# Attention of a hybrid trunk layer: value scale from column norms, bias shift as its own work, and a new table of work

## The chip, the cores and the metric

The kernel runs on one core of a Trainium2 chip. The metric is the device time of one execution in microseconds (us). The kernel before was timed three times: 1098.44, 1096.51 and 1096.65 us, a median of 1096.65 us. A separate profiled execution took 1097.14 us.

## The reference, cut to what matters

One layer is computed for two groups of tokens with shared weights: 128 context tokens and 512 latent tokens, 640 together, 1024 channels wide. The change lies in the attention of this layer:

```python
def block_attention(q, k, v):
    B, N, H, D = q.shape
    KV = k.shape[2]
    G = H // KV
    ...
        s = jnp.einsum('bqkgd,btkd->bkgqt', qblk, k).astype(jnp.float32) * scale
        p = jax.nn.softmax(s, axis=-1).astype(v.dtype)
        return jnp.einsum('bkgqt,btkd->bqkgd', p, v)
```

There are 16 query heads and 4 key/value heads of 64 channels. Context queries read the 128 context keys; latent queries read 512 latent keys and 128 cached ones. Before this stands the first projection (`u @ w_in`, with a normalisation of q and k per head and a rotary turn); behind it stand the output projections, a gated convolution and a feed-forward part. Those stages are not changed.

## The kernel before, in words

Every large product is made in three matmuls of rounded parts (high by high, high by low, low by high). The program runs in stages: a prologue that makes the keys and values of all 640 tokens; the attention; then the mixing stage, the feed-forward part and the output. Only the attention stage is changed. In the profile it begins at about 57.5 us, when the last products of keys and values end, and ends at about 243.1 us, when the first matmul of the next stage starts.

**Works.** The attention stage is written as a list of small pieces, each of them a `work` with a name, an engine, the works it must follow and the "rooms" it holds (a bank of PSUM, a slot of SBUF). The long string `PLAN` at the head of the file is the order: each entry is the number of a work, a letter for the engine where a work can run on one of several ("a" is the first), and digits that pick its rooms. `follow` issues the works in exactly this order, so each engine's instruction queue is fixed by the table; an engine never passes over an instruction that waits. `POOL_WAY` is a string of 32 digits; a "1" sends one subtraction (P2 of the second half of a step) to GpSimd (POOL), a "0" to VectorE (DVE).

**The pieces that the prediction speaks of**, by their names in the code:

- `q{g}{t}.{c}`: a quarter of the query projection for key/value head g and token tile t, six matmuls (line 687). `rot`, `sq`, `sum`, `factor`, `add`, `norm` (lines 818 to 865) make the rotary turn and the normalisation of a tile of q or k on DVE, ScalarE (ACT) and POOL; `turn` transposes it on PE (894, 1018), and `hi` and `lo` split the result (900, 903, 1020, 1022).
- `hi {u}` and `lo {u}`: the split of a weight unit (799, 804); each has two `lo` halves, on DVE or POOL.
- The **value scale**: every value channel is divided by a number of its own so that it fits 16-bit floats, and multiplied back at the end. `vmax` (910) takes the largest magnitude of each of the 256 channels over 768 tokens per partition; `v turn` (917) transposes; `v col` (921 to 923) takes the maximum over partitions and its reciprocal; `v spread` (930) and `v row` (932) spread it over all partitions; `v back` and `v un` (939, 945 to 947) keep the inverse; `v scale` (959), `v hi` (965) and `v lo` (968) make the 16-bit parts of the values, in thirds. All three `v hi` wait for all three `v scale`, since the parts lie on the values' own memory.
- A **step** n (36 of them, for g, t and half of the four heads): `s{n}` makes scores on PE (1057) in one PSUM "area" per head (three areas exist, A of two banks each); `max{n}.{h}` (1104, with the shift of the bias at 1106 for the second head) on DVE; `exp` (1109) and `P1` (1115) on ACT; `P2` (1120, 1122) on POOL or DVE; `T` (1126) a transposing DMA from the SP queue; `pv{n}` (1143, 1151) the product with the values on PE. On the POOL way `exp` writes to an SBUF slot E, so the area is free after `exp`; on the DVE way the area stays held until `P2` has read it.
- `R`, `O`, `AH`, `AL` (1163 to 1173) finish a pair of steps. `gate0` and `gate1` are products of the next stage that fill PE at the end.

Of the kernel before, what the change touches and what calls it, by code (L numbers as in the profile page):

```python
# [52 lines left out]
49a 113a 66a 119a 353a5 63a 50a 61a 64b 120a 109a01 39a 138a 121a 40a 110a 359a21 62a 100a 124a1 204a 114b 140a 115a1 135a0 360a
101a 116a2 139b 117a 361a 136a 125a 365a 102a1 206b 275a 362a2 141a 122a12 103a3 366a0 142a 126a 104a 205a 354a1 144a2 363a 123a
281a 367a4 372a01 143a0 127a 355a0 364a0 145a 356a 146a 128a4 378a 357a 151a0 129a0 147a 358a 379a1 152a 130a 368a 373a 389a21
380a3 370a 374a 381a 369a1 148a1 395a 153a 375a1 390a 149a1 154a 382a2 396a0 376a 157a0 150a 391a 402a10 377a3 155a21 397a0 400a
383a 156a 158a 371a1 392a2 408a 398a 403a 164a0 409a1 393a 159a 404a 399a4 165a 410a4 413a 419a02 160a 405a3 394a5 411a 384a
406a 425a 407a0 161a3 385a2 166a 420a 162a3 426a0 386a 167a 412a1 163a 387a 421a 432a21 388a 168a10 427a1 430a 401a1 169a 433a
170a1 422a0 428a 438a 434a 177a0 423a 439a1 429a2 178a 171a 435a2 443a 172a 449a01 440a3 436a 424a3 173a 414a 455a 441a 437a4
450a 456a0 174a4 179a 175a2 415a1 176a 457a4 180a 416a 442a5 462a12 417a 458a 181a02 451a 418a 183a2 463a 431a1 452a1 182a 459a0  # L60
453a 464a 190a0 468a 465a0 454a1 479a0 184a 469a1 466a 444a 185a 480a 470a2 467a2 186a 491a21 473a 445a0 460a 481a 446a 471a
191a 497a 447a 482a 472a3 492a 192a 483a3 498a0 448a 193a 484a 493a 187a1 485a4 194a21 504a10 188a0 499a4 502a 189a 195a 196a0
461a1 505a 500a 494a1 510a 506a 474a 495a 501a5 511a 207a0 197a 475a2 515a 198a 507a0 476a 496a0 208a 477a 508a 512a2 199a 478a
210a 521a21 509a1 513a 276a 211a 486a1 527a 212b 514a2 200a2 487a0 522a 201a1 277b 213a 528a1 488a 202a 214a 489a 875a 278b
529a3 490a 534a10 215a1 523a 530a 879a 216a1 503a1 532a 524a4 535a 531a3 540a 536a 516a 525a 541a0 223a0 217a 517a1 545a 218a
542a1 518a 551a20 526a4 519a 537a0 219a 520a 224a 557a 543a 220a1 552a 225a 558a1 538a 221a3 544a0 226a 559a2 222a 564a01 229a2
560a 553a 539a5 227a02 533a1 565a 554a3 228a 570a 566a 561a1 236a0 555a 571a0 237a 230a 567a4 562a 575a 231a 581a21 556a2 572a1
568a 232a 546a 582a 573a 569a3 587a 583a 233a2 238a 547a0 234a2 548a 588a1 239a 235a 574a4 549a 594a01 240a21 584a0 550a 589a2
241a 585a 563a1 242a0 590a 595a 586a0 611a2 600a 596a 249a0 591a5 612a 601a0 576a 243a 597a3 592a 605a 244a 602a4 598a 250a
577a2 245a 613a 599a1 578a 623a10 603a 251a 579a 629a 615a1 604a2 580a 252a 630a1 616a 246a1 255a1 624a 617a3 636a20 247a0 631a0  # L70
253a10 625a 632a 642a 593a0 626a2 248a 637a 606a 643a 254a 633a4 634a 256a 638a 627a 262a1 257a 607a1 647a 628a0 614a 644a3 608a
263a 258a 609a 645a 639a4 259a3 264a 610a 260a1 646a5 640a 282a 618a0 261a 653a02 284a 641a1 619a2 620a 283b 265a 621a 659a 883a
622a 660a0 654a 279a0 268a2 666a12 876a 266a00 269a 267a 655a 635a1 672a 270a 661a1 877a 648a 656a0 667a 271a 673a1 280a 878b
664a 657a 649a1 674a2 272a4 650a 658a2 285a 662a 273a3 651a 274a 668a 286a 652a 887a 675a 683a02 288a0 677a 663a3 669a3 287a2
289a 295a1 684a 290a 888a0 689a 685a 291a 296a 676a0 670a 690a0 889a 686a4 694a 696a12 691a0 687a 671a4 692a 297a 697a 292a2
702a 698a 298a 688a1 890a 293a2 299a12 699a1 294a 891a 301a1 300a 700a 703a1 693a5 308a1 302a 892a 707a 713a01 704a2 303a 678a0
304a 719a 705a 714a 720a0 665a 701a0 715a 726a21 679a0 706a4 724a 716a3 680a 309a 732a 681a 721a4 682a 310a 733a 717a 722a 305a0
311a 727a 718a2 306a0 734a0 743a0 307a 314a2 735a 695a0 728a 723a3 312a01 729a1 708a 744a 313a 736a1 730a 745a 321a1 315a 737a
755a12 316a 731a5 709a2 746a 747a2 710a 322a 317a 761a 711a 712a 323a 762a1 756a 318a0 324a 748a 763a3 319a1 768a20 749a0 764a
325a20 757a 320a 327a0 766a 758a4 738a0 774a 326a 765a4 769a 775a0 725a 759a 770a 750a1 328a 760a1 739a1 779a 329a 771a0 740a  # L80
785a01 751a2 772a 741a 330a 776a1 742a 773a5 331a4 791a 777a 334a0 332a3 786a 792a1 335a 333a 778a2 787a 752a 798a12 793a2 796a
336a 753a 804a 794a 880a 754a 337a 805a0 799a 881b 795a3 767a1 338a10 788a3 806a4 789a 882b 780a 340a1 800a 790a0 341a 807a
815a20 781a1 809a 801a0 782a 893a0 342a 339b 808a1 783a 816a 884a 894a 821a 343a 817a 885b 784a 895a 822a1 802a 344a1 886b 896a
818a1 803a4 826a 345a2 828a10 819a 823a2 346a 897a 820a2 824a 797a1 834a 829a 835a0 898a0 825a5 830a 845a20 836a3 839a 810a
831a4 846a 837a 832a 847a 899a 851a 833a0 811a2 900a 848a0 812a 901a 852a1 849a 838a3 813a 858a10 856a 853a1 814a 902a 854a
850a1 827a1 864a 859a 865a 903a2 855a4 860a 840a 866a2 869a 861a4 867a 904a 841a1 862a 911a 868a2 905a 842a 843a 863a5 906a 844a
857a0 907a 908a 870a 909a 871a0 872a 873a 910a 874a
"""
POOL_WAY = "11111111101111111011111011111110"
# [20 lines left out]
def trunk_layer(ctx, tc, x_prompt, x_sample, cache_k, cache_v, c, c_ctx, w_ada, b_ada, g_pre1, g_post1, g_pre2,  # L110
# [614 lines left out]
    with tc.tile_pool(name="att", bufs=1) as at:  # L725
# [147 lines left out]
        for t in range(NT):  # L873
# [28 lines left out]
            def k_lo(kh=kh, kl=kl, pk=pk):  # L902
# [3 lines left out]


        vsum, vsq = vcol[:, 0:2], vcol[:, 2:4]
        vz = Room(any_of("X", NX))
        big = work("vmax", "DVE", lambda: V.tensor_reduce(out=slot(XS, vz), in_=VV.rearrange("p s c -> p c s"), axis=AX.X, op=ALU.max,  # L910
                                                                          apply_absolute_value=True), list(v_copies.values()), [vz])
        pv_ = Room(ANY)

        def v_turn():
            p = at_bank(pv_, 256)
            for i in range(2):
                PE.transpose(p[:, i * 128:(i + 1) * 128], slot(XS, vz)[:, i * 128:(i + 1) * 128], ident)
# [1437 lines left out]
```

## Time and profile before

| what | value |
|---|---|
| median of three runs | 1096.65 us |
| the profiled execution, its own time | 1097.14 us |
| its span, first to last instruction | 1095.3 us |
| TensorE (PE) matmul busy | 1075.9 us (98%) |
| DVE busy | 858.6 us (78%) |
| ACT busy | 580.9 us (53%) |
| POOL busy | 130.4 us (12%) |
| granted TensorE clock, mean | 0.997 |
| attention stage | about 57.5 to 243.1 us of the span |

Times in the views are counted from the first instruction of the program. A row of the timeline gives start, duration, engine, line, operation, written tile <- read tiles, and behind it in brackets idle time of the engine and who ended it. A row of stretches gives busy time of each engine in a stretch (and the number of instructions), then the granted TensorE clock, the mean share of the DMA engines that was busy, and GB/s. A row of groups gives busy time and the mean duration in ns of instructions with one line and shape. A busy PE is not PE at its peak: the ends of its matmuls are modelled, and two that follow each other overlap.

### The profile page before, as it was taken

Reading aid. Unit: us, or ns where it says so; the run is one execution under the profiler, and the core shown is the slowest. Engines: PE = TensorE matmul, PEld = TensorE weight load, DVE = VectorE, ACT = ScalarE, POOL = GpSimd, SP = SyncE. Lnnn points to the kernel's source line nnn. Section 1 sums busy time; section 2 is a strip of 40 time slices with the busy share of each in tenths; the row PEclk is TensorE's granted clock in tenths of the full one; section 3 lists DMA queues with packets and bytes.
Section 4 is the critical chain, followed back from the end, with each engine's and each line's share of the span. In section 5 each row is a group of like instructions: output and inputs, shape, how many; then the busy total and the mean of one; then the engine's idle time right before and its main releaser. Section 6 shows DMA issues by size and latency. Waiting matters only on the chain.

```text
span 1095.3 us, 20378 instructions
## 1 busy us (share of the span) xinstructions
PE 1075.9 (98%) x8133; PEld 998.4 (91%) x8133; DVE 858.6 (78%) x1316; ACT 580.9 (53%) x1047; POOL 130.4 (12%) x161
## 2 busy tenths in 40 slices
PE   8999999999999999999999999999999999999997
PEld 6788888889999999999999789999999999998886
DVE  5698988856479889987488468889989988989544
ACT  5458987862344454445423266655556455545442
POOL 1077655620000000000000021000000000000001
PEclk9999999999999999999999999999999999999999
DMA  9828999898234333233445634234434433335722
GB/s 321 246 71 145 181 172 169 153 179 223 72 101 123 109 97 92 78 97 97 130 142 190 196 135 136 91 100 128 129 113 128 139 103 107 122 102 194 268 82 96
DMA packets 245613, 152.18 MB, mean 139 GB/s; under 512 B 94602, under 2 KB 224134, under 8 KB 245518
## 3 DMA queue, kind: packets, MB, share of 16 engines
q1 hardware_dynamic: 245406, 150.84, 50.3%
q8 instruction: 64, 1.05, 0.4%
q14 instruction: 31, 0.25, 0.1%
q10 hardware_dynamic: 112, 0.04, 0.0%
HBM read 117.39 MB, written 11.44 MB: 118 GB/s over the span
## 4 chain that ended last, share of the span: by engine, by line
PE 78%; ACT 1%; DVE 1%; DMA 0%; SPq 0%; issue 0%; POOL 0%; DVEq 0%; ACTq 0%
PE b L1255 46%; PE b L232 10%; PE b L234 10%; PE b L233 10%; PE b L1874 1%; DMA PT<-P 0%; PE b L287 0%; SPq L1126 0%; PE b L1724 0%; DVE marks L1104 0%; ACT P L1115 0%; ACT E L1109 0%; PE s L687 0%; PE b L350 0%; ACT s L1109 0%
## 5 line engine op out<-in xcount | busy, mean ns | idle before, releaser
L1255 PE MATMUL b<-ZBr,whi 128*128 128x320 f32 x688 | 152.2, 309 | 0.0
L1255 PE MATMUL b<-MT,whi 128*128 128x320 f32 x608 | 134.2, 309 | 0.0
L1255 PEld LDWEIGHTS b<-ZBr,whi 128*128 128x128 f32 x688 | 115.0, 188 | 0.1
L1255 PE MATMUL b<-ZBr,wlo 128*128 128x320 f32 x344 | 106.2, 309 | 0.0
L1255 PEld LDWEIGHTS b<-MT,whi 128*128 128x128 f32 x608 | 101.6, 188 | 0.0
L1255 PE MATMUL b<-MT,wlo 128*128 128x320 f32 x304 | 94.0, 309 | 0.0
L1242 ACT ACTIVATE whi<-SUM 128x1024 fp32r<-128x1024 f32 x40 | 42.2, 1055 | 78.4 <-DVE SUM L1789 75.9
L1819 DVE SCALAR_TENSOR_TENSOR Y<-C,cffn,Y 128x642 f32<-128x642 f32 x88 | 77.9, 885 | 0.9
L1255 PE MATMUL b<-ZBT,whi 128*128 128x320 f32 x320 | 71.0, 309 | 0.0
L1255 PE MATMUL b<-UL,whi 128*128 128x320 f32 x228 | 70.8, 311 | 0.0
L1255 PE MATMUL b<-UH,wlo 128*128 128x320 f32 x228 | 70.1, 307 | 0.0
L1242 ACT ACTIVATE whi<-WB 128x1024 fp32r<-128x1024 f32 x38 | 40.1, 1055 | 55.9 <-DVE WB L1356 55.9
L1255 PE MATMUL b<-UH,whi 128*128 128x320 f32 x228 | 69.7, 306 | 0.0
L1246 DVE TENSOR_TENSOR wlo<-raw,whi 128x1024 fp32r<-128x1024 f32 (+1 forms) x51 | 50.4, 1020 | 21.8 <-ACT whi L1242 21.8
L198 DVE TENSOR_TENSOR wlo<-raw,whi 128x1024 fp32r<-128x1024 f32 (+1 forms) x31 | 34.2, 1103 | 41.1 <-ACT whi L197 40.6
L1255 PEld LDWEIGHTS b<-ZBr,wlo 128*128 128x128 f32 x344 | 64.6, 188 | 0.0
L1263 ACT ACTIVATE p<-b 128x320 f32<-128x320 f32 x78 | 34.2, 439 | 54.8 <-PE b L1255 53.0
L1255 PEld LDWEIGHTS b<-MT,wlo 128*128 128x128 f32 x304 | 57.1, 188 | 0.0
L1255 PEld LDWEIGHTS b<-ZBT,whi 128*128 128x128 f32 x320 | 54.2, 188 | 1.5
L1104 DVE TENSOR_REDUCE marks<-s 128x1 f32<-128x640 f32 x64 | 51.5, 816 | 4.4 <-PE s L1057 4.4
L1246 DVE TENSOR_TENSOR wlo<-WB,whi 128x1024 fp32r<-128x1024 f32 x38 | 46.5, 1223 | 8.7 <-ACT whi L1242 8.6
L1242 ACT ACTIVATE whi<-raw 128x1024 fp32r<-128x1024 f32 (+1 forms) x51 | 43.5, 892 | 18.0 <-PE b L234 10.3
(422 smaller groups left out, 3220.4 us busy)
## 6 DMA issues: line engine op xcount, KB each, us to landing
raw<-in_w_in_dram SPq DMA_DIRECT2D x48, 512.0 KB
RAW<-in_w_up_dram SPq DMA_DIRECT2D x40, 512.0 KB
raw<-in_w_down_dram SPq DMA_DIRECT2D x22, 512.0 KB
actd<-Y SPq DMA_DIRECT2D x18, 321.0 KB
ada<-in_w_ada_dram SPq DMA_DIRECT2D x10, 512.0 KB
XT<-in_w_ada_dram SPq DMA_DIRECT2D x9, 512.0 KB
raw<-in_w_att_out_dram SPq DMA_DIRECT2D x8, 512.0 KB
raw<-in_w_conv_out_dram SPq DMA_DIRECT2D x8, 512.0 KB
```

The source lines that it names most:

```text
L198: V.tensor_tensor(out=lo[:, :n], in0=raw, in1=hi[:, :n].bitcast(F32), op=ALU.subtract)
L232: PE.matmul(out, ah, bh, start=start, stop=False)
L233: PE.matmul(out, ah, bl, start=False, stop=False)
L234: PE.matmul(out, al, bh, start=False, stop=stop)
L1104: V.tensor_reduce(out=mk[:, h:h + 1], in_=s_of(), axis=AX.X, op=ALU.max, negate=True)
L1242: S.activation(to[0], raw, AF.Copy)
L1246: V.tensor_tensor(out=lo, in0=raw, in1=hi.bitcast(F32), op=ALU.subtract)
L1255: PE.matmul(out, p[:, ws], q[:, k, :], start=start and k == 0 and n == 0, stop=stop and k == 3 and n == 2, skip_group_check=True)
L1263: S.activation(t, pair[j][b], AF.Copy)
L1819: V.scalar_tensor_tensor(out=y, in0=crows(j)[i][:, d:d + NACT], scalar=cffn[:, 44 * d + o:44 * d + o + 1], in1=y, op0=ALU.mult, op1=ALU.add)
L1874: PE.matmul(dn["pms"][t], acts(k)[1][i][:, c0:c0 + 128], w[h], start=False, stop=n == 2 and k == NJ - 1)
```

## The change

Three things are changed, all in the attention stage.

1. The value scale of a channel is no longer the reciprocal of its largest magnitude but of the root of its sum of squares. `vmax` and `v turn` go. In their place stand three `v square` on ACT (each squares a third of the values, 512 elements per partition, into a slot P), three `v total` on PE (each four matmuls of 128 channels against two columns of ones), a smaller `v col` on DVE that adds the six sums of a channel and keeps them off zero, and `v factor` on POOL, a power of -0.5. The reciprocal in `v col` goes. Everything from `v spread` on stays.
2. The shift of the bias is a work of its own, `shift{n}`, on DVE; `exp{n}.1` follows it.
3. `PLAN` is a new table for the 949 works there are now (912 before), with new choices of engines and rooms, and `POOL_WAY` sends 26 subtractions to POOL (28 before).

```diff
-POOL_WAY = "11111111101111111011111011111110"
+POOL_WAY = "11111111101111011111111101111000"
...
-        vz = Room(any_of("X", NX))
-        big = work("vmax", "DVE", lambda: V.tensor_reduce(out=slot(XS, vz), in_=VV.rearrange("p s c -> p c s"), axis=AX.X, op=ALU.max,
-                                                                          apply_absolute_value=True), list(v_copies.values()), [vz])
         pv_ = Room(ANY)
-
-        def v_turn():
-            p = at_bank(pv_, 256)
-            for i in range(2):
-                PE.transpose(p[:, i * 128:(i + 1) * 128], slot(XS, vz)[:, i * 128:(i + 1) * 128], ident)
-        vt = work("v turn", "PE", v_turn, [big], [pv_, vz])
+        tops = []
+        for i in range(3):
+            vz = Room(any_of("P", NP_))
+
+            def square(i=i, vz=vz):
+                S.activation(slot(PS, vz).bitcast(F32)[:, 0:512].rearrange("p (s c) -> p s c", s=2), VV[:, 2 * i:2 * i + 2, :], AF.Square)
+
+            def total(i=i, vz=vz):
+                p, x = at_bank(pv_, 24), slot(PS, vz).bitcast(F32)
+                for k in range(4):
+                    c = 4 * i + k
+                    PE.matmul(p[:, 2 * c:2 * c + 2], x[:, k * 128:(k + 1) * 128], ones[:, 0:2], start=True, stop=True, skip_group_check=True)
+            a = work(f"v square {i}", "ACT", square, [v_copies[t] for t in ((1,), (2, 3), (4, 0))[i]], [vz])
+            tops.append(work(f"v total {i}", "PE", total, [a], [vz, pv_]))
 
         def v_col():
-            V.tensor_reduce(out=vsum, in_=at_bank(pv_, 256).rearrange("p (i c) -> p i c", i=2), axis=AX.X, op=ALU.max)
+            p = at_bank(pv_, 24).rearrange("p (s i two) -> p i s two", i=2, two=2)[:, :, :, 0]
+            V.tensor_reduce(out=vsum, in_=p, axis=AX.X, op=ALU.add)
             V.tensor_scalar(out=vsum, in0=vsum, scalar1=1e-30, scalar2=None, op0=ALU.max)
-            V.reciprocal(vsq, vsum)
-        vc = work("v col", "DVE", v_col, [vt], [pv_])
+        vc = work("v col", "DVE", v_col, tops, [pv_])
+        vc = work("v factor", "POOL", lambda: G.tensor_tensor(out=vsq, in0=vsum, in1=mhalf[:, :2], op=ALU.pow), [vc])
...
                         V.tensor_reduce(out=mk[:, h:h + 1], in_=s_of(), axis=AX.X, op=ALU.max, negate=True)
-                        if h:
-                            V.tensor_scalar(out=mk[:, 1:2], in0=mk[:, 1:2], scalar1=SHIFT * math.log(2), scalar2=None, op0=ALU.add)
+
+                    def shifted(mk=mk):
+                        V.tensor_scalar(out=mk[:, 1:2], in0=mk[:, 1:2], scalar1=SHIFT * math.log(2), scalar2=None, op0=ALU.add)
                     mx = work(f"max{n}.{h}", "DVE", most, [sc], [ar[h]])
+                    if h:
+                        mx = work(f"shift{n}", "DVE", shifted, [mx])
```

The table moves works on every engine. Three places matter for the prediction. In the rows below stand the line, the operation, the written tile <- the read tiles, and the size; the changed file's lines are 2 higher up to `v scale`'s chain, 8 higher in the chain and the scores, and 11 higher behind the shift.

**VectorE, around the value column (`v col`).** Before, `vmax` (L910) comes tenth in the stage, and `v col` (L921 to L923) three works behind it:

```order
L847 TENSOR_REDUCE ssqs<-Z_731 128x4
L910 TENSOR_REDUCE X_732<-VV 128x256
L847 TENSOR_REDUCE ssqs<-Z_729 128x4
L855 TENSOR_TENSOR PT_724<-P_721,rk 128x512
L921 TENSOR_REDUCE vcol<-s_102_840 128x2
L922 TENSOR_SCALAR vcol<-vcol 128x2
L923 RECIPROCAL vcol<-vcol 128x2
```

Now `v col` (L929, L930) stands behind the rotation, the sums and the additions of the third query tile:

```order
L824 TENSOR_TENSOR X_734<-s_94_755,tabq 128x256
L825 TENSOR_TENSOR QF_737<-s_94_755,tabq 128x256
L845 TENSOR_TENSOR QF_736<-QF_736,X_733 128x256
L849 TENSOR_REDUCE ssqs<-Z_730 128x4
L1030 TENSOR_TENSOR QT_738<-s_98_808,QT_738 128x256
L867 TENSOR_TENSOR QF_736<-QF_736,rq 128x256
L845 TENSOR_TENSOR QF_737<-QF_737,X_734 128x256
L929 TENSOR_REDUCE vcol<-s_103_914 128x2
L930 TENSOR_SCALAR vcol<-vcol 128x2
```

What moved: the column of sums is the 29th work of VectorE in the stage, where it was the 13th.

**GpSimd, the value chain.** Before, GpSimd does one `v scale` (L959) and one `v lo` (L968) of three:

```order
L855 TENSOR_TENSOR PT_727<-P_720,rk 128x512
L959 TENSOR_TENSOR P_722<-VV,vrow 128x512
L843 TENSOR_TENSOR QF_737<-QF_737,X_732 128x256
L850 TENSOR_TENSOR rq<-ssqs,mhalf 128x4
L968 TENSOR_TENSOR VV<-P_721,VV 128x512
```

Now it does the power (L932), all three `v scale` (L967) and all three `v lo` (L976):

```order
L867 TENSOR_TENSOR QF_737<-QF_737,rq 128x256
L932 TENSOR_TENSOR vcol<-vcol,mhalf 128x2
L852 TENSOR_TENSOR rq<-ssqs,mhalf 128x4
L967 TENSOR_TENSOR P_722<-VV,vrow 128x512
L967 TENSOR_TENSOR P_719<-VV,vrow 128x512
L967 TENSOR_TENSOR P_718<-VV,vrow 128x512
L845 TENSOR_TENSOR QF_735<-QF_735,X_732 128x256
L976 TENSOR_TENSOR VV<-P_719,VV 128x512
L976 TENSOR_TENSOR VV<-P_718,VV 128x512
L976 TENSOR_TENSOR VV<-P_722,VV 128x512
```

What moved: two thirds of the scaling and of the low parts went from VectorE to GpSimd, in a row.

**TensorE, from `s2` to `s3`.** The scores write PSUM areas (`s_...` with a number). Before, `s3` writes one area that `s2` had (s_102_840) and one that it had not, and a turn and projection pieces (L687) stand between them:

```order
L1057 MATMUL s_102_840<-KH,QT_739 128x320
L1018 MATMUL s_104_927<-ident,QF_736 128x128 x2
L687 MATMUL s_94_755<-whi_829,UH 128x256
L687 MATMUL s_94_755<-wlo_830,UH 128x256
L687 MATMUL s_94_755<-whi_829,UL 128x256
L1057 MATMUL s_104_927<-KH,QT_741 128x320
L1057 MATMUL s_102_840<-KH,QT_741 128x320
```

Now `pv0` and a turn alone (L1154, L1162, L1026) stand between `s2` and `s3`, and `s3` writes both areas of `s2`:

```order
L1065 MATMUL s_103_914<-KH,QT_740 128x320
L1065 MATMUL s_99_839<-KH,QT_740 128x320
L1154 MATMUL s_98_808<-ident,marks 64x128 x4
L1162 MATMUL s_98_808<-PT_728,VV 64x128
L1026 MATMUL s_102_859<-ident,QF_735 128x128 x2
L1065 MATMUL s_103_914<-KH,QT_739 128x320
L1065 MATMUL s_99_839<-KH,QT_739 128x320
```

What moved: ahead of `s3` 26 projection pieces stood in TensorE's queue, and 22 stand there now; and its two areas are both the ones that `s2` filled last, one of them on the way on which the area is held until VectorE's `P2`.

More of the change, by code (lines that the diff above doesn't have):

```diff
@@ L53 @@
[L53 to L56, printed above, removed]
@@ new lines @@
+360a2 384a 381a0 120a2 369a0 121a3 128a 385a 382a 386a1 132a 361a 383a1 387a2 396a21 390a 122a 144b 362a 209a 363a 133a2 388a
+280a 397a 146a 134a0 402a 398a 147a 210b 389a3 403a 156a1 135a 399a4 148a1 404a1 157a 400a 374a 158a 405a1 408a 401a2 410a01
+149a1 406a 150a 159a 416a 375a4 211b 169a0 417a 162a2 411a 418a0 170a 151a 160a00 407a5 412a 428a21 163a 161a 413a0 422a 152a
+391a1 434a 419a2 286a 164a 435a 414a 377a 436a1 165a 429a 415a1 437a4 442a01 420a 392a1 430a 393a 171a 443a 394a 438a 431a3
@@ new lines @@
+801a4 808a 823a 771a 824a0 802a 925a1 825a3 817a 803a5 335a 830a10 783a 818a 826a 336a0 809a0 836a 819a0 926a 337a2 828a 347a
+837a 927a 820a 838a1 827a3 928a 338a 348a 839a1 831a 848a20 929a 840a 832a 821a2 349a0 854a 833a4 797a1 350a3 842a 855a 834a
+856a0 811a 841a1 351a 857a2 849a 862a10 812a0 858a 850a 813a 835a4 930a0 814a 860a 868a 851a3 931a 869a 852a 870a 859a0 932a
+815a 933a 871a0 863a 829a1 872a 864a 853a5 865a1 874a 880a20 934a 866a 843a 873a2 881a 886a 882a 935a0 887a 867a3 844a1 936a
```

68 lines of the change are left out of this document (33 added, 35 removed).

## The prediction

> **What bounds the kernel now.** I read the page first, for the engine that the end follows:
>
> ```profile
> span 1095.3 us, 20378 instructions
> PE 1075.9 (98%) x8133; PEld 998.4 (91%) x8133; DVE 858.6 (78%) x1316; ACT 580.9 (53%) x1047; POOL 130.4 (12%) x161
> ```
>
> PE is busy nearly all the time and nothing but attention changes, so what counts is when PE gets through the attention stage. The stretches of that stage come next:
>
> ```profile
> 57.55:100.00 42.45, 39.43 (x351) 34.65 (x351) 40.56 (x91) 28.14 (x69) 35.31 (x35) 0.96 0.48 99
> 100.00:140.00 40.00, 38.82 (x559) 33.90 (x560) 34.88 (x77) 35.15 (x83) 24.39 (x24) 1.00 0.94 175
> 140.00:180.00 40.00, 38.17 (x531) 33.58 (x529) 35.05 (x78) 34.51 (x82) 23.80 (x24) 1.00 0.91 166
> 180.00:220.00 40.00, 38.26 (x543) 34.41 (x543) 33.47 (x75) 34.57 (x83) 23.11 (x22) 1.00 0.97 166
> ```
>
> After the length stand PE, weight loads, DVE, ACT, POOL; then the clock, the DMA share. There are two regimes. In the opening DVE is busy 40.56 of 42.45 us and POOL 35.31, while DMA has half its time free: DVE bounds it. From 100 us on PE is busy about 96%, the DMA engines 91 to 97%, DVE and ACT 84 to 88%: four resources nearly full, with little room to make up a delay. The opening also holds the only slow clock of the stage:
>
> ```profile
> 62.00:65.40 3.40, 1.75 (x15) 1.34 (x14) 3.40 (x3) 1.12 (x2) 3.40 (x5) 1.00 0.18 41
> 65.40:68.80 3.40, 3.39 (x16) 2.79 (x15) 3.33 (x8) 0.77 (x2) 2.46 (x3) 0.50 0.00 0
> ```
>
> PE was busy 1.75 of 3.4 us, and for the next 3.4 us it was granted half its clock: 1.7 us of PE work lost. It cost little there, as DVE was full throughout.
>
> **The change part by part.** The removed and the moved value work:
>
> ```profile
> 61.69 2.83 DVE L910 TENSOR_REDUCE X<-VV 128x256 f32<-128x1536 f32 x1
> 64.67 0.41 PE L917 MATMUL s<-ident,X 128*128 128x128 f32 x2 [0.93 <-DVE X L910]
> 66.42 0.41 DVE L921 TENSOR_REDUCE vcol<-s 128x2 f32<-128x256 f32 x1
> 67.07 0.17 DVE L923 RECIPROCAL vcol<-vcol 128x2 f32<-128x2 f32 x1
> 69.19 0.63 PE L939 MATMUL s<-ident,vrow 128*64 128x2 f32 x16
> L965 ACT ACTIVATE VV<-P 128x512 f16<-128x512 f32 x3 | 1.8, 624 | 0.0
> L850 POOL TENSOR_TENSOR rk<-ssqs,mhalf 128x4 f32<-128x4 f32 x5 | 5.1, 1026 | 0.0
> L959 DVE TENSOR_TENSOR P<-VV,vrow 128x512 f32<-128x512 f32 x2 | 2.2, 1106 | 0.0
> L968 DVE TENSOR_TENSOR VV<-P,VV 128x512 f16<-128x512 f32 x2 | 1.6, 790 | 0.0
> 76.86 1.72 POOL L959 TENSOR_TENSOR P<-VV,vrow 128x512 f32<-128x512 f32 x1
> 80.84 1.17 POOL L968 TENSOR_TENSOR VV<-P,VV 128x512 f16<-128x512 f32 x1
> ```
>
> DVE loses `vmax` (2.83), the reciprocal (0.17), two `v scale` (2.2) and two `v lo` (1.6): 6.8 us, all in the stretch that it bounds. Its new column reduces 12 numbers; between the 0.17 of the reciprocal and the 0.41 of the old one I take 0.2. But DVE takes two key additions over from POOL, one more query addition, and two `P2`; POOL takes the power (1.03), two `v scale` at 1.72 and two `v lo` at 1.17, 6.8 us more. POOL's 35.31 of 42.45 us have just that room. ACT's three squares, like the 512-element row, are 3 x 0.62 = 1.9 us; they lie in the 14 us that ACT is idle in the opening and cost at most 1.9 if that cover went. The twelve small matmuls are not in the trace: eight of 2 columns show 16 records in 0.63 us, so I take 24 records, 0.95 us, with 0 and 1.9 us (twice that pace) as ends; `v turn` gives 0.41 back.
>
> `shift` is the same instruction as before:
>
> ```profile
> L1106 DVE TENSOR_SCALAR marks<-marks 128x1 f32<-128x1 f32 x32 | 4.9, 154 | 1.1
> L1120 POOL TENSOR_TENSOR P<-E,P 128x640 f16<-128x640 f32 x28 | 39.4, 1409 | 20.7 <-ACT P L1115 20.7
> L1120 DVE TENSOR_TENSOR P<-s,P 128x640 f16<-128x640 f32 x4 | 3.3, 820 | 0.6 <-ACT P L1115 0.5
> ```
>
> In 24 of 32 steps it still stands right behind its maximum; in 8 one work lies between, at most 0.82 us long. I take 0; the ends are 0 and 8 x 0.82 = 6.6 us, were each of them on the path.
>
> **The opening, walked through.** Does the relief of DVE reach PE? In the new order 29 works stand before `v col` on DVE. The rows that price them:
>
> ```profile
> 57.88 0.42 DVE L823 TENSOR_TENSOR P<-s,tabk 128x256 f32<-128x256 f32 x1
> 58.21 0.75 DVE L847 TENSOR_REDUCE ssqs<-Z 128x4 f32<-128x260 f32 x2
> 64.78 1.72 DVE L855 TENSOR_TENSOR PT<-P,rk 128x512 f32<-128x512 f32 x1
> 73.60 0.67 DVE L903 TENSOR_TENSOR KL<-s,KH 128x512 fp32r<-128x512 f32 x1
> 74.98 0.69 DVE L855 TENSOR_TENSOR PT<-P,rk 128x512 f32<-128x512 f32 x1
> L804 DVE TENSOR_TENSOR wlo<-raw,whi 128x512 fp32r<-128x512 f32 x6 | 4.1, 685 | 0.0
> L843 DVE TENSOR_TENSOR P<-P,X 128x256 f32<-128x256 f32 x1 | 1.3, 1264 | 0.0
> L843 DVE TENSOR_TENSOR QF<-QF,X 128x256 f32<-128x256 f32 x1 | 0.6, 636 | 0.0
> ```
>
> Rotations, sums and small differences start 0.33 us apart: 24 of them, 7.9 us. Four large differences at 0.6 make 2.4, five additions at 0.64 to 1.26 make 3.2 to 6.3, two key norms at 0.69 to 1.72 make 1.4 to 3.4. That is 14.9 to 20.0 us. POOL mostly works on four-element powers meanwhile, so I take 16: `v col` begins at 57.55 + 16 = 73.5, seven us later than before.
>
> Behind it come: 0.6 to its end, then the power (1.03) on POOL while DVE makes the last key differences (1.2) that `s0` waits for; `v spread` stands behind `s0` on PE (1.2 + 0.6 us), then `v row` (0.39): 78.0. Three `v scale` on POOL, one after another: 78.0 + 3 x 1.72 = 83.1. All `v hi` wait for the last one, and on ACT's queue behind two of them stands `exp1.1`, which frees the area that `s2` needs: 83.1 + 1.2 + 1.0 = 85.3. Meanwhile PE runs out of pieces. Before, `s2` and `s3` began here:
>
> ```profile
> 88.00 0.66 PE L1143 MATMUL s<-ident,marks 128*64 128x128 f32 x8
> 88.92 0.41 PE L1057 MATMUL s<-KH,QT 64*128 64x320 f32 x2
> 91.22 0.28 PE L687 MATMUL s<-wlo,UH 128*128 128x256 f32 x1
> 91.34 0.28 PE L687 MATMUL s<-whi,UL 128*128 128x256 f32 x1
> 91.91 0.67 PE L1057 MATMUL s<-KH,QT 64*128 64x320 f32 x2
> 92.86 0.75 ACT L1109 ACTIVATE s<-s,marks 128x640 f32<-128x640 f32 x1
> 93.75 0.70 ACT L1115 ACTIVATE P<-s 128x640 f16<-128x640 f32 x1
> 95.09 0.81 DVE L1122 SCALAR_TENSOR_TENSOR P<-s,P 128x640 f16<-128x640 f32 x1
> ```
>
> `s2` now starts 3.5 us earlier than its 88.92. But `s3` wants both areas of `s2`, one of them held until `P2` has read it. Behind `exp1.1` stand on ACT the last `v hi`, one `P1`, a square, `exp1.0`, its `P1`, `exp2.0`, a spread and `P1 2.0`: eight works, 5.3 us at 0.62 to 0.75 us each with the shorter square and spread, to 90.6; then `P2` 0.8: `s3` at 91.5. PE has `pv0` and a turn to do between 86.6 and then, some 1.1 us. So `s3` comes 0.4 us earlier, yet with four projection pieces fewer done; a piece is six matmuls 0.12 apart, 0.7 us, so 2.8 us of PE work is still owed. Net **2.4 us behind**; if the additions run at their fast ends (1 us earlier) 1.4, at their slow ends 6.
>
> **The clock.** PE then idles about 4 of 5 us, more than the idle that led to the half clock above. I expect another 3.4 us at half clock, now just when PE has work owed: **1.7 us**; the ends are 0 and 3.4 (two such stretches). [...]
>
> **The end.** `P2` of steps 33 and 34 goes from POOL (1.41) to DVE (0.82), 0.6 us sooner for the last transposes:
>
> ```profile
> 240.14 1.03 PE L1151 MATMUL s<-PT,VV 128*64 128x128 f16 x30 [0.52 <-DMA PT<-P]
> PE s L1151 <- DMA PT<-P: 2.3, 4, 0.7
> ```
>
> The last products on PE waited 0.5 us for them, all products 2.3 us. I take **-0.5** for the end, and **-1.1** (half of the rest and a little from the scores) since most `pv` stand further behind their `s` in PE's new queue; ends 0 and -4.
>
> **The sum:** 2.4 + 1.7 - 0.5 - 1.1 = +2.5 us on the profiled 1097.14 (span 1095.3 and 1.8 around it): 1099.6. The profiled execution lies 0.5 above the median 1096.65, so I forecast **1099.2** for the runs; its own range, 1097 to 1102.
>
> **Rivals.** (1) *DVE's relief goes through: faster.* DVE's net loss of work is about 4 us (6.8 off; two key additions, a query addition and two `P2`, 3.5 to 4.8, on, less two halves of a weight's low part at 0.69). If the middle follows DVE's queue and not PE's debt, all later maxima come 4 us sooner: 1092.7. For it speaks 40.56 of 42.45 us; against it, that PE and DMA are fuller than DVE from 100 us on, and that POOL's value chain eats the gain ahead of `s2`. It decides if `s3` starts before 90.5 and no half clock follows. [...] (3) *POOL takes over: slower still.* The 6.8 us come before the `P2` of steps 1 to 4 in its queue; if these come some 5 us late, both slots E stay full and the `exp` behind them, then the `s`, wait: 1097 + 5 = 1102, up to 1105. Against it: POOL idles 15 of 40 us after 100. [...]
>
> **How the numbers follow.** Forecast 0.44, (1) 0.26, (2) with (4) 0.19, (3) 0.11. A measurement of this kernel can tell about 0.2%, 2.2 us, from no change. Faster: (1), 0.26. Within: (2) and the part of the forecast below 1098.8, 0.05: 0.24. Slower: 0.50. The range, 1092.5 to 1104.5, reaches to (1) on one side and through most of (3) on the other.
>
> **What would show it.** `v col` at about 73.5 and its six later links; `s2` at 85 to 87; PE idle ahead of `s3` on DVE's `P2`; a granted clock of 0.5 near 91 to 95; POOL full from 75 to 105; afterwards a stretch from `s3` to the end no shorter than the old 151 us. I am wrong if `s3` begins by 90 with the clock full, or if the middle's `pv` and `s` wait so much less that the stage ends before 242 us.

## The result, and the profile after

The changed kernel takes 1094.45 us (median of 7 runs, 1093.41 to 1095.50), the kernel before beside it 1097.04 us (7 runs, 1096.51 to 1099.37): a ratio of 0.9972, 95% interval 0.9960 to 0.9984. It is faster by 2.6 us where the forecast was slower by 2.5. The profiled execution took 1094.45 us.

The top of the page of the changed kernel:

```profile
span 1092.6 us, 20419 instructions
PE 1073.0 (98%) x8155; PEld 998.1 (91%) x8155; DVE 852.3 (78%) x1313; ACT 584.8 (54%) x1050; POOL 130.9 (12%) x163
```

Its stretches, columns as in the prediction:

```profile
57.55:100.00 42.45, 38.81 (x346) 36.00 (x344) 34.82 (x84) 29.64 (x70) 36.31 (x35) 0.96 0.45 97
100.00:140.00 40.00, 38.66 (x593) 34.41 (x589) 35.29 (x79) 35.80 (x82) 25.96 (x27) 1.00 1.02 182
140.00:180.00 40.00, 38.84 (x543) 34.59 (x542) 34.48 (x78) 35.64 (x83) 25.36 (x26) 1.00 1.05 173
180.00:220.00 40.00, 38.19 (x571) 34.09 (x569) 34.81 (x77) 37.40 (x88) 24.10 (x23) 1.00 1.07 178
```

DVE fell from 40.56 to 34.82 us in the opening: it is no longer full throughout. From 100 to 220 us PE is shown as busy as before (115.7 against 115.3 us), but the three stretches hold 1707 matmul records instead of 1633. The projection pieces among them are as many as before; the rest is above all 60 more matmuls of the `pv`, 29.2 us of them instead of 26.9. A share of busy time does not say how much work is done.

The value chain in the timeline, on PE, DVE and POOL:

```profile
68.39 0.95 PE L923 MATMUL s<-ones,P 128*128 128x2 f32 x8
69.45 1.84 PE L923 MATMUL s<-ones,P 128*128 128x2 f32 x16
71.44 0.16 DVE L929 TENSOR_REDUCE vcol<-s 128x2 f32<-128x12 f32 x1
72.25 0.70 POOL L932 TENSOR_TENSOR vcol<-vcol,mhalf 128x2 f32<-128x2 f32 x1
76.66 3.75 POOL L967 TENSOR_TENSOR P<-VV,vrow 128x512 f32<-128x512 f32 x3
```

The totals are 24 records in two rows, 2.8 us of PE. `s1` to `s4`, in the timeline of the changed kernel (of each step only its first row):

```profile
78.72 0.41 PE L1065 MATMUL s<-KH,QT 64*128 64x320 f32 x1
84.13 0.42 PE L1065 MATMUL s<-KH,QT 64*128 64x320 f32 x2
87.32 0.44 PE L1026 MATMUL s<-ident,QF 128*128 128x128 f32 x2 [1.11 <-DVE P L1133]
88.10 0.81 DVE L1133 SCALAR_TENSOR_TENSOR P<-s,P 128x640 f16<-128x640 f32 x1
88.97 0.59 PE L1065 MATMUL s<-KH,QT 64*128 64x320 f32 x2 [1.21 <-DVE P L1133]
95.67 0.42 PE L1065 MATMUL s<-KH,QT 64*128 64x320 f32 x2
```

and the same two ends in the kernel before:

```profile
82.36 0.93 PE L1057 MATMUL s<-KH,QT 64*128 64x320 f32 x2
95.56 0.80 PE L1057 MATMUL s<-KH,QT 64*128 64x320 f32 x2 [0.46 <-ACT E L1109]
```

`s1` starts 3.6 us earlier, with two pieces fewer and one turn more ahead of it (2 x 0.7 less 0.2 us): PE is 2.4 us ahead, 0.3 of it from before the stage. In the stretches where the kernel before waited for `vmax` and then had its half clock, PE is now nearly full, at the full clock:

```profile
62.00:65.40 3.40, 3.24 (x28) 2.93 (x27) 3.36 (x9) 2.86 (x5) 3.40 (x5) 1.00 0.02 5
65.40:68.80 3.40, 3.40 (x33) 3.40 (x31) 3.25 (x8) 1.39 (x4) 3.32 (x4) 1.00 0.17 39
```

`s3` starts 2.9 us earlier, with four pieces and one turn fewer done (3.0 us): PE is level, 0.1 us behind. `s4` starts 0.1 us later, with one piece and one turn fewer done (0.9 us): PE is 1.0 us behind. Ahead of the turn of q03 and of `s3` it waits for DVE's `P2`, as foretold, and then gets 3.4 us of half clock, from 90.24 us on:

```profile
85.80:89.20 3.40, 1.07 (x18) 0.68 (x15) 3.37 (x8) 3.35 (x9) 3.32 (x5) 1.00 0.23 46
86.83:90.24 3.41, 1.71 (x15) 1.28 (x15) 2.90 (x8) 3.36 (x10) 3.33 (x5) 1.00 0.52 97
90.24:93.65 3.41, 3.41 (x17) 3.41 (x17) 2.44 (x6) 3.32 (x7) 3.41 (x4) 0.50 1.02 235
```

The stage's last projection matmul, before and after:

```profile
242.81 0.31 PE L687 MATMUL s<-UH,wlo 128*128 128x320 f32 x1
```

```profile
239.06 0.31 PE L689 MATMUL s<-UH,wlo 128*128 128x320 f32 x1
```

So from `s4` on the stage is 4.75 us shorter (1.0 behind, 3.75 ahead). The whole stretch from `s4` to that matmul, before and after, in one row each:

```profile
95.56:242.81 147.25, 141.01 (x1991) 124.63 (x1992) 119.28 (x262) 121.47 (x283) 78.90 (x74) 1.00 0.95 167
```

```profile
95.67:239.06 143.39, 138.42 (x2000) 124.09 (x2000) 117.44 (x258) 121.97 (x280) 78.64 (x77) 1.00 1.03 174
```

PE idles 5.0 us there instead of 6.2, which is 1.3 us of the 4.75. The other 3.5 us are busy time: PE is busy 2.6 us less although it does one piece and one turn (0.9 us) more. The means of its matmuls are nearly the same, so in the new order they follow each other more closely. Of the 3.75 the span keeps 2.7; most of the rest is lost at 436 us, where PE meets a transfer and DVE that did not come earlier:

```profile
433.76 1.95 DVE L343 SCALAR_TENSOR_TENSOR XG<-XG,s 128x768 f32<-128x768 f32 x2 [1.52 <-DMA XG<-in_w_ada_dram]
436.26 0.53 PE L1266 MATMUL b<-MT,whi 128*128 128x320 f32 x2 [0.34 <-DVE WA L1277]
```

### The profile page after: what moved, and what is told of

Read it like the earlier page. It is cut to its first block, busy times and chain, and to the rows that moved or that the text cites. A ratio compares the mean times of both kernels' runs of the same rounds, so it can differ in the third digit from the quotient of the medians.

```text
span 1092.6 us, 20419 instructions
## 1 busy us (share of the span) xinstructions
PE 1073.0 (98%) x8155; PEld 998.1 (91%) x8155; DVE 852.3 (78%) x1313; ACT 584.8 (54%) x1050; POOL 130.9 (12%) x163
## 4 chain that ended last, share of the span: by engine, by line
PE 87%; DVE 5%; DMA 4%; ACT 2%; issue 1%; POOL 0%; DVEq 0%; SPq 0%; ACTq 0%
PE b L1266 44%; PE b L234 10%; PE b L236 10%; PE b L235 10%; PE s L689 5%; PE s L1065 2%; PE s L1162 1%; DMA PT<-P 1%; DVE marks L1112 1%; DMA araw<-in_w_ada_dram 1%; PE s L234 1%; DMA raw<-in_w_in_dram 1%; DVE wlo L1257 1%; PE s L236 1%; PE s L235 1%
```

## The experiments

All times: median, ratio to the kernel before on the same chip with its 95% interval, and the mean granted clock over all runs of the kernel.

| run | median us (runs) | ratio | mean clock |
|---|---|---|---|
| before (beside x1 to x18) | 1097.63 (87) | | 0.9984 |
| changed | 1094.45 (7) | 0.9972 [0.9960, 0.9984] | 0.9969 |
| x1 after_max | 1095.96 (11) | 0.9992 [0.9981, 1.0002] | 0.9956 |
| x8 max_late | 1098.11 (12) | 0.9997 [0.9985, 1.0008] | 0.9936 |
| x2 before_norm | 1102.31 (5) | 1.0039 [1.0026, 1.0052] | 0.9956 |
| x3 opening_before | 1108.72 (4) | 1.0094 [1.0079, 1.0110] | 0.9912 |
| x4 opening_after | 1111.26 (4) | 1.0126 [1.0112, 1.0140] | 0.9922 |
| x5 fill | 1091.98 (5) | 0.9942 [0.9930, 0.9954] | 0.9990 |
| x9 fill_kept | 1092.11 (5) | 0.9950 [0.9938, 0.9963] | 0.9986 |
| x16 fill_spread | 1091.75 (5) | 0.9952 [0.9939, 0.9964] | 0.9986 |
| x17 old_fill | 1096.87 (11) | 0.9997 [0.9988, 1.0006] | 0.9985 |
| x18 max_filled | 1094.51 (7) | 0.9971 [0.9960, 0.9982] | 0.9970 |
| x6 pieces | 1095.22 (6) | 0.9970 [0.9959, 0.9981] | 0.9968 |
| x7 shift_joined | 1094.15 (5) | 0.9968 [0.9956, 0.9980] | 0.9976 |
| x13 tail_pool | 1094.61 (11) | 0.9976 [0.9967, 0.9985] | 0.9968 |
| x15 old_pool_way | 1095.11 (10) | 0.9977 [0.9967, 0.9986] | 0.9972 |
| x10 switch | 1094.38 (9) | 0.9970 [0.9960, 0.9979] | 0.9976 |
| x11 noswitch | 1095.21 (8) | 0.9975 [0.9964, 0.9986] | 0.9975 |
| x12 pv_nearer | 1122.85 (4) | 1.0222 [1.0205, 1.0239] | 0.9908 |
| x14 old_pv_later | 1120.96 (4) | 1.0207 [1.0188, 1.0225] | 0.9942 |

Edits of the order are shown by names of works; where a work moved into a slot or bank that was taken, it got another free one.

### Order or value scale?

```diff
 x1: PLAN of the changed kernel
-v square 0..2 (ACT), v total 0..2 (PE), v factor (POOL)
+vmax (DVE, at the last square), v turn (PE, at the last total), v col with reciprocal
 x2: PLAN of before
-vmax, v turn
+v square 0, 1 (ACT); v total 0, v square 2, v total 1, 2; v factor behind v col
 x8: as x1
+vmax (DVE) behind q01 add; v turn behind q03.3; v col behind k0 lo
```

> The changed kernel with its order, shift works and POOL_WAY kept, and only the value scale put back to the maximum: vmax on DVE where the last square stood on ACT, the old transpose on PE where the last total stood, the old v col with its reciprocal, no factor on POOL. Theory O (the gain lies in the new order of the middle, from s4 on): within 1 us of the changed kernel, 1093.5 to 1095.5. Rival R (the gain is DVE's relief in the opening): DVE gets 2.8 us back there, so 2 to 3 us slower than the changed kernel, 1096.5 to 1097.5.

> The kernel before with its order kept, and only the value scale by channel norms: three squares on ACT where vmax stood (into E slots), three totals on PE where the transpose stood, v col, factor on POOL right behind it. Theory O: no gain, 1096 to 1098. Rival R: DVE loses 2.8 us in the stretch that it bounds, 1094 to 1095.

> As the kernel in which the changed kernel's order had the maximum, but with vmax on DVE behind the addition of q01 (after the key turns are fed), the transpose on PE behind q03.3 and v col behind the low part of k0. Theory R (DVE's 2.8 us count wherever they stand): 2 to 3 us slower than the changed kernel, 1096.5 to 1097.5. Rival P (only the place ahead of the key norms cost it): within 1 us of the changed kernel, 1094 to 1095.5.

With the maximum the new order is not shown to be faster than the kernel before, in either place of `vmax`. x1, at 1095.96, lies between theory O and rival R; x8, at 1098.11, lies 0.6 above theory R's range and 2.6 above rival P's. With the norms the old order is slower by 0.4%, which neither theory expected: DVE waits for an addition of POOL, and then in `v col`, in its old place, for the totals (timeline of x2), and 6.8 us at half clock follow from 67 us on:

```profile
63.31 0.69 DVE L856 TENSOR_TENSOR PT<-P,rk 128x512 f32<-128x512 f32 x1 [1.64 <-POOL P L844]
65.96 0.17 DVE L928 TENSOR_REDUCE vcol<-s 128x2 f32<-128x12 f32 x1 [1.95 <-PE s L922]
```

So neither half of the change gains by itself here. The traces say where each counts. From `s4` to the last projection matmul x1 and x8, with the maximum in the new order, take 143.8 us each (99.54 to 243.30, 99.25 to 243.09), the changed kernel 143.4; the old order takes 147.25 in the kernel before and 148.1 with the norms (x2, 98.27 to 246.34). The shorter middle thus comes with the order, whatever the value scale. But x1 and x8 reach `s4` 3.9 and 3.6 us later than the changed kernel (0.8 and 0.5 of it from before the stage), and that eats the gain. What the maximum does there is seen in the stretches of x8:

```profile
72.20:75.60 3.40, 1.54 (x12) 1.12 (x10) 3.40 (x7) 0.38 (x1) 1.57 (x2) 1.00 0.00 0
75.60:79.00 3.40, 2.85 (x20) 2.12 (x20) 3.12 (x9) 0.83 (x3) 1.11 (x3) 0.68 0.09 21
79.00:82.40 3.40, 3.40 (x27) 3.38 (x28) 2.86 (x5) 2.64 (x10) 3.40 (x3) 0.50 0.42 140
82.40:85.80 3.40, 3.22 (x23) 2.46 (x23) 2.75 (x8) 2.10 (x3) 2.27 (x4) 0.81 0.08 17
```

PE waits behind `vmax`, and 6.8 us at half clock follow (0.32, 0.50 and 0.19 of 3.4 us are missing, 3.4 us of work), besides the one behind `s3`. The runs of one kernel differ by the clock in the same way: x8's twelve go from 1094.45 us at 0.996 to 1100.30 at 0.991. A straight line within each kernel gives 0.80 us (standard error 0.07) for each 0.001 of mean clock over 96 runs of 12 kernels in the new order (x5 left out), and 0.19 us (0.09) over 98 runs in the old one. 0.001 is 1.1 us of PE at full speed: by these lines the new order passes most of a lost clock on to the end, the old one little. A line is no test, though: in x8's stretches above, waits cost time and clock together. And the mean also counts a half clock at the very end, behind the last products (in the changed kernel's profile from 1090.3 us of 1092.6 on, worth 0.001), where there are no products left to slow down; it is worth 0.0004 to 0.0018 in the profiles.

With these slopes the means, taken to a clock of 1, give rough estimates (too low by about 0.8 us in the new order and 0.2 in the old, since that end is at half clock in every profile): before 1097.4 (1097.71 - 1.55 x 0.19), x1 1093.2, x8 1092.7, changed 1091.9 (1094.38 - 3.1 x 0.80). By them the order with the maximum is worth 4.2 to 4.7 us and the norms another 0.8 to 1.3; the clock gives back 3.5 in x1, 5.1 in x8 and 2.5 in the changed kernel. By the same estimate, that the norms spare half clock is the larger part of what they bring against x8, and somewhat under half against x1.

### The half clock

Twenty idle matmuls, whose results nobody reads, where PE waits ahead of `s3`:

```diff
+def fill(n):
+    out = bank_of(state["pz", 1, 0].at[0][1])[:, 256:512]
+    for _ in range(n):
+        PE.matmul(out, UH[:, 0, 0:128], UH[:, 0, 0:256], start=True, stop=True, skip_group_check=True)
 x5: fill(9) behind pv0, fill(11) behind the turn of q03
 x9: start=False, stop=False
 x16: x9, and v total 1 behind q03.0
 x17: before, fill(7) behind q01.1, fill(9) behind the turn of k0 (in q01's bank)
 x18: x8 with the fills of x9, and 12 behind v turn
```

> The changed kernel with 20 matmuls more, whose results nobody reads: 9 behind pv0 and 11 behind the turn of q03, into the unused half of a bank, where PE waits 1.2 and 1.5 us anyway. Theory C (the idle of PE ahead of s3 brings the half clock at 90 to 94 us, and the 1.7 us it costs are carried to the end): granted clock 1.00 from 86 to 96 us, time 1.7 us less than the changed kernel, 1092 to 1093.5. Rival M (the middle makes up what the opening loses): clock may be full, time as the changed kernel, 1094 to 1095.

> The changed kernel with the same 20 idle matmuls as in the run before, but none of them starts a new sum, so that the open sum of q10 in the same bank stays whole. Theory C: no half clock from 86 to 96 us, stage 2 to 3 us shorter than the changed kernel's, 1091 to 1093 and faster than both kernels. If the earlier run was short only because it broke that sum: 1094 to 1095.

> The kernel with the 20 idle matmuls that start no new sum, and besides with the last v total behind q03.0 instead of ahead of it, so that two of the three runs of tiny matmuls do not follow each other (in the profile of the kernel with the idle matmuls alone a half clock of 1.7 us still came behind them, at 70 to 75 us). Theory C: fewer such stretches in the mean, 0.5 to 1.5 us less: 1090.7 to 1091.8. Rival (v col comes later by q03.0's 0.7 us and that is carried to the end): 1092 to 1092.8.

> The kernel before with 16 idle matmuls (7 behind q01.1, 9 behind the turn of k0, results unread, none starts a new sum) where PE waits 0.9 and 1.2 us in its opening. Theory C holds for the old order too: the half clock at 65 to 69 us goes and the time falls by 1.7 us, 1095 to 1096. Rival (what the prediction said of it: it costs little there, since DVE is full throughout): granted clock 1.00 in the opening, time as before, 1096.7 to 1097.7.

> The changed kernel's order with the maximum (vmax on DVE behind the addition of q01), and with 32 idle matmuls: 12 behind the transpose of the maxima, 9 behind pv0, 11 behind the turn of q03. Theory C (in this order the maximum costs only through the half clock that PE's waits bring): as the changed kernel with its 20 idle matmuls, 1091.5 to 1093. Theory R (DVE's 2.8 us are a delay by themselves): 1094 to 1096.

In x5 the starts fall into the bank in which q10's sum is open, and the first output comes out with a relative error of 0.28; x9, without starts, leaves it whole, and its time is the same (1092.11 against 1091.98). The stretches of x9 where the changed kernel had its half clock, and ahead of them:

```profile
68.80:72.20 3.40, 3.40 (x27) 3.40 (x27) 2.82 (x10) 0.40 (x2) 3.08 (x5) 0.81 0.00 0
72.20:75.60 3.40, 3.40 (x23) 3.40 (x22) 1.37 (x3) 0.60 (x1) 0.60 (x1) 0.68 0.00 0
85.80:89.20 3.40, 3.40 (x45) 3.06 (x44) 2.89 (x6) 3.31 (x8) 3.21 (x4) 1.00 0.01 2
89.20:92.60 3.40, 3.40 (x31) 3.08 (x31) 2.89 (x8) 3.35 (x8) 3.32 (x4) 1.00 0.82 155
```

The clock is kept behind `s3`, and the kernel is 2.3 us faster than the changed one (1092.11 against 1094.45; 0.9950 against 0.9972 of the kernel before), with a mean clock higher by 0.0017: theory C holds, and rival M, that the middle makes up such a loss, falls. x9 and x16 beat both kernels. In this execution another half clock came at 70 to 75 us, behind the totals, although PE is shown full there; x16, made against it, ends just inside theory C's numbers but cannot be told from x9 (the intervals overlap), so that step is open.

In the old order the same remedy changes nothing (x17), though it did keep the clock in its profile:

```profile
62.00:65.40 3.40, 2.41 (x20) 2.13 (x20) 3.40 (x3) 0.86 (x2) 3.40 (x4) 1.00 0.19 43
65.40:68.80 3.40, 2.50 (x26) 1.93 (x24) 3.33 (x9) 0.77 (x2) 2.46 (x3) 1.00 0.00 0
```

DVE is full there (3.40 and 3.33 of 3.40 us), and PE waits in both stretches. But over all runs the mean clock did not rise either (0.9985 against 0.9984), so x17 does not test how much the half clock of the old order costs; that it is little rests on the slope of 0.19 us. x18 gains 3.6 us on x8 with the fills, but its 1094.51 lies in theory R's range: its profile still has 6.8 us at half clock at 79 to 86 us, and to a clock of 1 it comes to 1092.4, 1.2 above x9's 1091.2. Both theories have a share.

The fix by real work instead of idle matmuls failed:

```diff
 x6: PLAN of the changed kernel
-lo 11 (POOL, twice, behind pv0 and the turn of q03)
+lo 11 (DVE, twice, behind q04 rot); q10.2, q10.3 (PE) behind pv0
```

> The changed kernel with both halves of the low part of weight unit 11 on DVE right behind the rotation of q04 (83.6 us) instead of on POOL (86.2 and 89.0), and with pieces q10.2 and q10.3 on PE ahead of the turn of q03, where PE idles. Theory C (what is lost at s3 is carried to the end): 1.4 us of pieces into the gap, and no half clock: 1.4 to 3.1 us less than the changed kernel, 1091.3 to 1093. Rival M: as the changed kernel, 1094 to 1095.

It is about as fast as the changed kernel (1095.22). The pieces filled the first gap, but `s3` still waited for `P2` (PE busy 1.99 of 3.40 us in the next stretch), and the half clock came all the same.

### What makes the middle shorter?

Spliced orders:

```diff
 x3: before up to s4, then the changed order for what is left
 x4: the changed kernel up to s4, then before's order for what is left
```

> The kernel before up to s4 (maximum, its order, its POOL_WAY), and from there the changed kernel's order and POOL_WAY for all works that are left. Theory O: it keeps the 1.7 us by which before was ahead at 94 us and gets the changed kernel's shorter middle (5.4 us shorter, of which 1.1 is given back after the stage): about 1097.0 - 5.4 + 1.1 = 1092.7, 1091.5 to 1094. Rival R: as before, 1096.5 to 1097.5.

> The changed kernel up to s4 (norms, its order, its POOL_WAY), and from there the order and POOL_WAY of before. Theory O: the debt of 1.7 us at 94 us stays and the middle is the old one: 1098 to 1099.5, which is where the forecast lay. Rival R: as the changed kernel, 1094 to 1095.

Both are far outside either theory: 11 to 14 us slower than before. In x4 the seam alone costs some 7 us (`s4` starts at 96.07, `s5` only at 107.45; the two stand 4.3 us apart before, 3.4 after), in x3 the loss comes later, so they do not tell opening from middle. They do show that one order's opening does not fit the other's middle.

Single parts of the change, put back:

```diff
 x7: shift{n} right behind max{n}.1 in all steps
 x13: POOL_WAY tail
-1000
+1110
 x15: POOL_WAY
-11111111101111011111111101111000
+11111111101111111011111011111110
```

> The changed kernel with each shift right behind its maximum, as before; it stands elsewhere in 8 of 32 steps. My term was 0: 1094 to 1095. Rival: the split is part of the gain, 8 x 0.15 us of DVE ahead of a later maximum: 1095 to 1096.

> The changed kernel with the second parts P of steps 33 and 34 (their head 1) on POOL again, as before. My term for the end was 0.5 us (0.6 us longer instructions ahead of the last transposes): 1095 to 1095.5, the stage 0.5 us longer between s33 and its end. Rival: POOL's lone instructions run beside DVE's and the end does not move: 1094 to 1094.7.

> The changed kernel's order with the old table of which second parts P run on POOL (step 15 on POOL, 19 on DVE, 33 and 34 on POOL). If that table makes the middle shorter: 1 us or more slower than the changed kernel, 1095.5 to 1097. If only the order of the queues does: 1094 to 1095 but for the end's half us.

All three lie within 0.7 us of the changed kernel, inside the intervals: neither the split of the shift nor the table of `P2` shows an effect, though one of 1 us could hide there. x13 fell on its rival's range: the 0.5 us that the prediction took for the end are not seen.

The new order groups the projection pieces: counted in the two traces, they are entered from other work 40 times instead of 53. The first matmul of a run of pieces takes 0.20 to 0.22 us instead of 0.12. Is that a change of the array's mode, from 128 columns of weights to 64 and back?

```diff
 x10: in 25 joints between two pieces of a tile
+PE.matmul(x[0:64, 256:258], UH[:, 0, 0:64], UH[:, 0, 0:2], start=False, stop=False, tile_position=(0, 0), ...)
 x11: the same joints
+PE.matmul(x[:, 256:258], UH[:, 0, 0:128], UH[:, 0, 0:2], start=False, stop=False, ...)
```

> The changed kernel with one 2-column matmul of 64 columns of weights at tile position (0, 0) in each of 25 joints between two adjacent projection pieces of one tile (groups 1 to 3), result unread: PE changes from the full array to a half and back. Theory S (each such change costs PE 0.1 us; this is part of why the new order, with fewer of them, is shorter): 25 x 0.2 = 5 us over the control with the full array, about 1100. Rival (the longer first and last matmuls of a run of pieces have another cause, as the wait for an operand): within 1 us of the control.

> Control: the same 25 matmuls of 2 columns with 128 columns of weights and no tile position, so that PE stays in one mode. Each costs its own few hundredths: 1095 to 1096.5 by both theories.

The rows of one joint, first x10, then x11 (timeline of PE):

```profile
167.35 0.28 PE L689 MATMUL s<-whi,UL 128*128 128x256 f32 x1
167.47 0.17 PE L1014 MATMUL s<-UH 128*64 128x2 f32 x1
167.49 0.36 PE L689 MATMUL s<-whi,UH 128*128 128x256 f32 x1
167.69 0.28 PE L689 MATMUL s<-wlo,UH 128*128 128x256 f32 x1
```

```profile
167.37 0.28 PE L689 MATMUL s<-whi,UL 128*128 128x256 f32 x1
167.49 0.17 PE L1014 MATMUL s<-UH 128*128 128x2 f32 x1
167.51 0.36 PE L689 MATMUL s<-whi,UH 128*128 128x256 f32 x1
167.72 0.29 PE L689 MATMUL s<-wlo,UH 128*128 128x256 f32 x1
```

They are alike: the matmul behind a short one takes 0.20 us from start to start in x10 and 0.21 in x11, whether the short one has 64 columns of weights or 128, and x10 is no slower than x11. Theory S falls: with 64 of 128 columns no price shows here beyond the control's. The 25 x 0.11 us that either kernel adds to PE (0.03 + 0.20 - 0.12 each, 2.8 us in all) do not show in the time of x10 (1094.38), and 0.8 us of them at most in x11 (1095.21), within the intervals of about 1 us. So the runs do not show that 13 entries fewer, some 1.3 us, are what shortens the middle, and they are too coarse to exclude a part of it.

The last theory was the distance from a step's scores to its products:

```diff
 x12: the changed kernel, 26 of the pv's one or two works earlier on PE
 x14: before, 30 of the pv's one or two works later on PE
```

> The changed kernel with 26 of the pv's one or two works earlier on PE (estimated PE work between each s and its pv, summed: 494 us in the changed kernel, 451 here, 436 in the kernel before; changes of PE's mode 94, 96, 99). Theory D (the middle waits less since pv's stand further behind their s): 43/58 of the 4.5 us of waits come back: 1097 to 1098.5. Rival W (the distance is worth nothing, the waits went for another reason): 1094 to 1095.5.

> The kernel before with 30 of the pv's one or two works later on PE (estimated PE work between s and pv 473 us instead of 436; the changed kernel has 494). Theory D (the distance alone shortens the middle): 2 to 3 us faster than the kernel before, 1094.5 to 1095.5. Rival J (the middle of each order is fitted as a whole: every pv stands just where its transposes land and its bank comes free, and a shift either way costs): slower than the kernel before, 1099 or more.

x12 loses 28 us, seven times or more what theory D said; x14 loses 23, as rival J said. A part of both is clock: their means, 0.9908 and 0.9942, lie 0.0061 and 0.0042 below the kernels that they were made from, 6.7 and 4.6 us of PE. Where PE waits in each (view of PE's waits: us, times, longest), x12 first:

```profile
PE s L1064 <- DVE P L1132: 4.8, 4, 1.9
PE s L1064 <- ACT E L1119: 3.6, 3, 2.2
PE s L1153 <- DVE AL L1183: 3.1, 3, 1.3
```

```profile
PE s L1018 <- DVE AL L1176: 4.4, 5, 1.4
PE s L1057 <- DVE P L1125: 3.9, 6, 1.0
PE s L1057 <- ACT E L1112: 2.5, 5, 0.8
```

In both, `s`, and in x12 `pv` (L1153), in x14 turns (L1018), wait for an area or a bank that a late `P2`, `exp` or `AL` still holds. A likely account is that one `pv` too early or too late delays the next `s`, and with it everything that feeds the `pv`'s behind; the views show the waits, not this chain. The distance is not a quantity of which more is better. Which part of the order makes the new middle 4.75 us shorter stays open: the shift, the table of `P2` and the mode of the array do not account for it, and the rest could not be taken apart without breaking it.

## Why the prediction was wrong

| step | predicted | measured |
|---|---|---|
| `v col` begins | 73.5 | 71.44 |
| totals on PE | 0.95 us (0 to 1.9) | 2.8 us (0.95 + 1.84) |
| power on POOL | 1.03 us | 0.70 us |
| last `v scale` done | 83.1 | 80.4 (76.66 + 3.75) |
| `s2`, `s3` start | 85.4, 91.5 | 84.13, 88.97 |
| PE behind the kernel before, at `s3` | 2.4 us | 0.1 us |
| half clock near 91 to 95 | yes | 90.24 to 93.65 |
| lost by it up to `s4` | 1.7 us | 0.9 us (1.0 behind at `s4`) |
| `shift` | 0 | not seen (x7) |
| `s4` to the end of the stage | -1.6 (-0.5 and -1.1) | -4.75 |
| behind the stage | 0 | +1.1 (3.75 less 2.7) |
| sum at the profiled execution | +2.5 | -2.7 |

**The mechanism at `s3` was right**: PE runs out of pieces, waits for `P2`, and gets 3.4 us of half clock when work is owed; x9, without that, is 2.3 us faster.

**The step that failed most** is the -1.6 us for the middle and the end (-0.5 and -1.1), which measured -4.75. The prediction read the middle as "four resources nearly full, with little room to make up a delay", took its busy time as fixed, and let the new order save only part of the 2.3 us for which products waited. But the new middle is another schedule. Its idle time fell by 1.3 us, near the 1.6 foretold; 3.5 us more went out of PE's busy time, for which the sum had no term. That PE was busy 96% was no bound: nearly the same busy time from 100 to 220 us held 1707 matmul records instead of 1633. The prediction itself had named, as a sign of being wrong, a stage that ends before 242 us; it ended at 239.4. What in the order brings the matmuls closer together stays open.

**The step that failed first** is the debt of 2.4 us at `s3`, which measured 0.1. Its source is the time of DVE's queue up to `v col`: 16 us were taken for it and 13.9 passed. The five additions in it were priced at 0.64 to 1.26 us each from rows of the kernel before and took 0.42 each in the new one (L845). The last `v scale` was then done 2.7 us early (each took 1.25 us, not 1.72), and `s3` started 2.5 us early. (Longer totals did not matter: PE was 2.4 us ahead at `s1` all the same.) As for a delay that does arise, the sentence on little room holds in x1: there `s4` comes 3.9 us later than in the changed kernel (99.54 against 95.67), and `pv35` still 3.6 (239.74 against 236.14; 0.8 of both is from before the stage).

That the half clock of the old order cost little agrees with the slope of 0.19 us, but was not tested (x17).

**Rival 1** gave 1092.7 if `s3` started before 90.5 and no half clock followed. `s3` started at 88.97; the half clock followed; 1092.7 + 1.7 is 1094.4, the time measured, and without it x9 takes 1092.1. The match is luck. Its mechanism was that all later maxima come sooner by DVE's saved work; but `s4`, which the maxima of step 4 follow, starts at 95.67 against 95.56, no sooner, the gain arises behind it, and the middle is as short with `vmax` in the order (x1, x8).

**The gaps** ahead of the half clock were short: waits of 1.1 and 1.2 us, with PE busy 1.71 of the 3.41 us ahead of it, were enough to lose the clock here, and filling them kept it (1.00 from 85.8 to 92.6 us in x9).

## What to carry to other kernels

Compare two orders of work by what each engine gets done in a stretch, not by its share of busy time; a new schedule is not the old one plus a delay. Look at the matmuls' own spacing too, not only at what PE waits for: most of the gain here was in busy time. Ask of a lost clock whether PE owes work behind it: here it went to the end, and twenty unread matmuls in a known wait bought 2.3 us. Do not shift many works of one queue of a fitted order by themselves: 26 to 30 products moved by one or two places cost 23 to 28 us, while single parts put back cost under 1.

## What the hardware showed

- The half clock of the attention stage lasts 3.41 us in the records of the kernel before and of the changed one, and twice that in x2, x8 and x18. The three of x1 begin at 67.03, 80.68 and 94.34 us: each four times 3.41 us behind the one before it. In the 3.41 us just ahead of the half clock PE was busy 1.76 us in the kernel before and 1.71 in the changed one. Runs of one kernel spread with the clock: x8's differ by 5.9 us over a mean clock of 0.991 to 0.996.
- A half clock also came at 70.9 us of x9 and 72.5 us of x6, although PE is shown busy for the whole 3.41 us ahead of it. The totals of 2 columns stand there in the order; in the changed kernel's profile they take 2.8 us of PE from 68.39 us on, and nothing was lost behind them (clock 1.00 up to 90.24 us).
- With matmuls that start a new sum in the other half of the bank of q10's open sum the first output came out with a relative error of 0.28 (x5); with the same matmuls and no starts it stayed whole (x9).
- A full-width matmul behind a 2-column one starts its successor after 0.20 us (x10, 64 columns of weights) or 0.21 (x11, 128) instead of 0.12.
- In both profiles the rows of DVE, ACT and POOL (1302, 931 and 134 of their operations before, 1299, 934 and 136 after) stand in the order in which the kernel issues them, and PE's lines too: none ran ahead of one that waited.
